# First loads on one queue in order of need, epsilon of the norms on VectorE, another order in the last norm

## The chip, the cores and the metric

The kernel runs on one core of a Trainium2 chip. The metric is the device time of one execution in microseconds (us). The core has five instruction streams that run side by side and wait for one another by semaphores: PE (TensorE: weight loads and matmuls), DVE (VectorE), ACT (ScalarE), POOL (GpSimd) and SP (SyncE, which here only issues DMAs). ACT and POOL can issue DMAs too. All DMAs are carried by 16 DMA engines.

## The reference, cut to what matters

A network of two layers, float32, on 256 tokens of width 1024:

```python
def reference(x, ...):
    for l in range(2):
        mix = mixer_sublayer(x, ...)                 # proj = x @ w_in (1024 x 7696), three branches, w_branch, w_out
        x = layer_norm(ALPHA * x + mix, ln1_g, ln1_b)
        ff = square(relu(x @ w_ff1)) @ w_ff2         # 1024 x 4096 and back
        x = layer_norm(ALPHA * x + ff, ln2_g, ln2_b)
    return x

def layer_norm(x, g, b):
    xc = x - mean(x)
    return xc * rsqrt(mean(xc * xc) + 1e-5) * g + b
```

One of the three branches (the gMLP) has a layer norm of its own, over 512 columns, with the parameters `gmlp_ln_g` and `gmlp_ln_b`.

## The kernel before, in words

**Number format.** Each float32 product is made of three matmuls in a faster format (F32R). An operand is split into a rounded part `hi` and a rest `lo = x - hi`; the product is hi·hi + hi·lo + lo·hi. The split of a weight piece is one ACT instruction (`split_hi`, L115: `whi` <- raw) and one DVE instruction (`split_lo`, L120: `wlo` <- raw, `whi`); the split of the input is L975 on ACT and L976 on DVE (`split_x`, tile `actT`). ACT and DVE take their instructions strictly in the order in which the program writes them.

**Pieces and units.** All weights come as *pieces* of up to 128 x 1024 float32 (512 KB). A piece is loaded by one DMA on SP's queue (L106) into a ring of raw buffers (tile `wraw`, four of them, and in the beginning six more, tile `wearly`). A piece may be loaded once the piece that held its buffer has had its `lo` made. PE's work is a list of *units*, each of which uses one or two pieces; a plan fixes at which unit the `hi` and the `lo` of each piece are written into the streams of ACT and DVE.

**The first nine units** (`first_units`) multiply the input with the columns for `v` and `gv`, 1024 columns in all: 8 steps over k (128 rows of the weights each), 12 matmuls of 512 columns in each step (two outputs, two token tiles, three products). In step 0 the weights come as two pieces of 256 KB, in the others as one of 512 KB. In this text w0 to w8 are these nine pieces, x0 to x3 the four loads of the transposed input (`xT`; k = 0, k = 1, k = 2 and 3, k = 4 to 7; 128, 128, 256 and 512 KB). x0 to x3 are issued by ACT, w0 to w8 by SP. The splits stand in this order: on ACT x0, w0, w1, x1, w2, x2, w3, w4, x3, w5 to w8; on DVE x0, w0, w1, x1, x2, w2, w3, x3, w4 to w8. So of step 1 the `lo` of w2 stands behind both parts of x2.

PE begins with `keep_warm` (L136): nine float32 matmuls of 128 columns on zeros, which need no load. The profile counts each as two.

**Parameters.** `params_a` (L309 to L320) loads what a layer's gMLP and GLA branches need: `lngb` (the norm's g and b and a bias, one row of 1536 sent to all 128 partitions, 768 KB), `ws` (512 KB), `bg` (2 KB) and `nw` (64 KB). POOL issues them: for layer 0 as `start` of unit 1, for layer 1 as `start` of the unit near the end of layer 0 that first uses the last weights of w_ff2. They are first needed at L344 (`lngb`, DVE, after unit 8), L351 (`ws`) and later.

**Norms.** `residual_norm` makes the sum with the residual (L227) and the statistics (L228, L231) on DVE; then `rstd_of` adds epsilon (L208) and takes the power -0.5 (L209), both on POOL; meanwhile DVE makes (x - mean) * g in two halves (L235), and then, when the power is there, the product with it plus b (L243). The last norm of the program, for the second token tile, treats columns 768 to 1023 apart: ACT multiplies (L240) and POOL adds b (L241), so that three output DMAs are issued, two by SP and one by ACT (L245).

```python
    load_xT(0)            # L1047
    load_more(1)
    load_xT(1)
    load_more(2)
    for c in (2, 3):
        load_xT(c)
    load_more()
    splits(-1)
```

Of the kernel before, what the change touches and what calls it, by code (L numbers as in the profile page):

```python
# [14 lines left out]
OP = mybir.AluOpType  # L15
# [6 lines left out]
NT = 2  # L22
# [12 lines left out]
EARLY_PIECES = 20  # L35
SPLIT_BUFS = 9
LEAD = 7
WARM = 9


class Piece:
# [13 lines left out]
def block_kernel(ctx, tc, ins, out):  # L55
    nc = tc.nc
# [5 lines left out]
    def sbt(tag, width, name, bufs=1, dt=F32):  # L62
        if width % 128:
            return small.tile([128, width], dt, tag=tag, name=name, bufs=bufs)
        return sb.tile([128, width], dt, tag=tag, name=name, bufs=bufs)
# [4 lines left out]
    def v3(t, n):  # L70
        return t.rearrange("p (a b) -> p a b", a=n)
# [11 lines left out]
    xraw = [sbt(tag, D, "xraw") for tag in ("Rk", "Rq")]  # L83

    def load_xT(c):
        k0, k1 = XCH[c]
        nc.scalar.dma_start(v3(xraw[k0 // 4], 4)[:, k0 % 4:(k1 - 1) % 4 + 1, :], ins["xT"][:, k0:k1, :])


    pieces = []  # L90
    units = []
# [6 lines left out]
    def start_load(p):  # L98
        n = p.shape[0] * p.shape[1]
        r = rank[id(p)]  # L100
        if r < EARLY_PIECES and r % (RAW_BUFS + EARLY_RAW) < EARLY_RAW:
            c = r % (RAW_BUFS + EARLY_RAW) * 1024
            p.raw = v3(early[:, c:c + n], p.shape[0])
        else:
            p.raw = v3(sbt("wraw", 1024, "wraw", bufs=RAW_BUFS)[:, :n], p.shape[0])
        nc.sync.dma_start(p.raw, p.src)  # L106
# [26 lines left out]
    def keep_warm(n):  # L133
        warm = pbank("pw", "warm")
        for _ in range(n):
            nc.tensor.matmul(warm[:, :128], wtile, wtile, start=True, stop=True)  # L136

    keep_warm(WARM)
    ident = sbt("ident", 128, "ident")
# [13 lines left out]
    def late_consts():  # L153
        nc.gpsimd.memset(wgx.bitcast(F32), 0.0)
        nc.gpsimd.memset(lrx.bitcast(F32), 0.0)
        nc.gpsimd.memset(scan_mask, 1.0)
        for n in range(4):
            nc.gpsimd.memset(scan_mask[:, n * 64:n * 64 + 1], 0.0)
        nc.gpsimd.memset(moba_mask[:, 128:256], 1)
        yield  # L160
        for h in range(H):
            nc.vector.tensor_scalar(gla_mask[:, h * 128:(h + 1) * 128], jp, 0.0, None, op0=OP.is_ge)
            nc.vector.memset(gla_mask[0:64, h * 128 + 64:(h + 1) * 128], 0)
        for c0 in (0, 256):
            nc.vector.tensor_scalar(moba_mask[:, c0:c0 + 128], jp, 0.0, None, op0=OP.is_le)
        yield
# [38 lines left out]


    def rstd_of(dst, var, eps, n=1):
        nc.gpsimd.tensor_scalar(dst, var, eps, None, op0=OP.add)  # L208
        nc.gpsimd.tensor_tensor(dst, dst, half_c.to_broadcast([128, n]) if n > 1 else half_c, op=OP.pow)  # L209

    def transpose_split(src, dst_hi, dst_lo, t, half):
        p = pbank("pw", "pT")
        for k in range(4):
            nc.tensor.transpose(p[:, k * 128:(k + 1) * 128], src[:, (half * 4 + k) * 128:(half * 4 + k + 1) * 128], ident)  # L214
        sl = (slice(None), slice(half * 4, half * 4 + 4), slice(t * 128, (t + 1) * 128))
        nc.scalar.copy(dst_hi[sl], v3(p, 4))
        nc.vector.tensor_tensor(dst_lo[sl], v3(p, 4), dst_hi[sl].bitcast(F32), op=OP.subtract)

    def residual_norm(t, acc, lnp, dst, final=False):

        g, b = lnp
        xr = xres[t]
        st = sbt("st", 12, "st", bufs=2)
        mv = sbt("mv", 3, "mvar", bufs=2)
        for h in range(2):
            sl = slice(h * 512, (h + 1) * 512)
            nc.vector.scalar_tensor_tensor(xr[:, sl], xr[:, sl], ALPHA, acc[h], op0=OP.mult, op1=OP.add)  # L227
            nc.vector.bn_stats(st[:, h * 6:(h + 1) * 6], xr[:, sl])  # L228
            if h == 0:
                yield  # L230
        nc.vector.bn_aggr(mv[:, 0:2], st)  # L231
        rstd_of(mv[:, 2:3], mv[:, 1:2], LN_EPS)
        for h in range(2):
            sl = slice(h * 512, (h + 1) * 512)
            nc.vector.scalar_tensor_tensor(xr[:, sl], xr[:, sl], mv[:, 0:1], g[:, sl], op0=OP.subtract, op1=OP.mult)  # L235
        last = final and t == NT - 1
        for c0, c1 in ((768, 1024), (0, 512), (512, 768)) if last else ((0, 512), (512, 1024)):
            sl = slice(c0, c1)
            if c0 == 768:
                nc.scalar.activation(xr[:, sl], xr[:, sl], AF.Identity, scale=mv[:, 2:3])  # L240
                nc.gpsimd.tensor_tensor(xr[:, sl], xr[:, sl], b[:, sl], op=OP.add)  # L241
            else:
                nc.vector.scalar_tensor_tensor(xr[:, sl], xr[:, sl], mv[:, 2:3], b[:, sl], op0=OP.mult, op1=OP.add)  # L243
            if final:
                (nc.scalar if c0 == 768 else nc.sync).dma_start(out[0, t * 128:(t + 1) * 128, sl], xr[:, sl])  # L245
        yield
        if final:
            return
        yield
        yield  # L250
        hi, lo, _ = dst()
        for h in range(2):
            transpose_split(xr, hi, lo, t, h)
# [50 lines left out]
    def build_layer(l, xT):  # L304
# [4 lines left out]
        def params_a():  # L309
            rs = sbt("RS", 1536, "lngb")  # L310
            a = ins["gmlp_rows"][l]
            nc.gpsimd.dma_start(rs, bass.AP(tensor=a.tensor, offset=a.offset, ap=[[0, 128], [1, 1536]]))
            ws = sbt("RkT", 1024, "ws")
            nc.gpsimd.dma_start(ws, ins["gmlp_wg"][l])
            bg = sbt("bg", 4, "bg")
            nc.gpsimd.dma_start(bg, ins["b_gate"][l])
            nw = sbt("nw", 128, "nw")
            a = ins["gla_norm_w"][l]
            nc.gpsimd.dma_start(nw, bass.AP(tensor=a.tensor, offset=a.offset, ap=[[0, 128], [1, 128]]))
            st.update(lng=rs[:, :1024], bs=rs[:, 1024:], wst=ws[:, :512], wgraw=ws[:, 512:], bg=bg, nw=nw)  # L320

        def params_ln(which):
# [9 lines left out]
        def gmlp_v_post(t):  # L332
            v = st["v"]
            vs = v[:, t * 512:(t + 1) * 512]
            nc.scalar.activation(vs, st["ps_v", t], AF.Gelu)
            yield
            for _ in range(t if l == 0 else 6 - 4 * t):
                yield
            s6 = sbt("st", 12, "st", bufs=2)
            mv = sbt("mv", 3, "mvar", bufs=2)  # L340
            nc.vector.bn_stats(s6[:, 0:6], vs)
            nc.vector.bn_aggr(mv[:, 0:2], s6[:, 0:6])
            rstd_of(mv[:, 2:3], mv[:, 1:2], LN_EPS)
            nc.vector.scalar_tensor_tensor(vs, vs, mv[:, 0:1], st["lng"][:, 0:512], op0=OP.subtract, op1=OP.mult)  # L344
            yield
            nc.vector.scalar_tensor_tensor(vs, vs, mv[:, 2:3], st["lng"][:, 512:], op0=OP.mult, op1=OP.add)
            st["v_done"] = st.get("v_done", 0) + 1
# [516 lines left out]
        def fin_of(which, dst, final=False):  # L864
            def fin(t, hf):
                if hf == 0:
                    st["fin", t] = residual_norm(t, st["acc", which, t], st[f"ln{which}"], dst, final)
                next(st["fin", t])
                if hf == 1:
                    side.append(st["fin", t])  # L870
            return fin
# [106 lines left out]
    xT = x0T  # L978
    sts = []
    for l in range(L):  # L980
        xT, s = build_layer(l, xT)
        sts.append(s)
    units[1].start = sts[0]["params"]
    units[6].start = lambda: side.append(late_consts())
    units[sts[0]["glb_unit"]].start = lambda: side.append(rope_tables())
    for s in sts:
# [34 lines left out]
    def load_more(limit=1000):  # L1021
        while loaded[0] < min(limit, len(pieces)) and taken_by[loaded[0]] < taken[0]:
            start_load(pieces[loaded[0]])
            loaded[0] += 1
# [15 lines left out]
    def advance():  # L1040
        for g in list(side):
            try:
                next(g)
            except StopIteration:
                side.remove(g)

    load_xT(0)  # L1047
    load_more(1)
    load_xT(1)
    load_more(2)  # L1050
    for c in (2, 3):
        load_xT(c)
    load_more()
    splits(-1)
# [54 lines left out]
```

## Time and profile before

| what | us |
|---|---|
| median of 3 runs | 880.16 (879.46 to 882.21) |
| the profiled execution's own time | 879.06 |
| its span (first to last instruction) | 877.3 |
| PE busy in the span | 863.3 (98%) |
| DVE, ACT, POOL busy | 616.8, 467.5, 73.9 |
| PE idle from 60 to 860 us | 0.65 (busy 799.35 of 800) |
| last matmul to the end of the span | 8.4 |

The span is cut into stretches by time; a row of a stretch gives, after its length, how long each engine was busy in it (and in how many instructions), TensorE's granted clock as a share of full speed (PEclk), the share of the DMA engines' time and the GB/s that they moved. A busy PE can still be slow: its matmuls are pipelined, so the distance from one start to the next says more. The timeline lists instructions by start; in brackets is how long the engine was idle before one, and what ended that.

### The profile page before, as it was taken

To read this page: it belongs to the slowest core of one execution; us is meant where nothing else is said; L and a number is where in the kernel's file an instruction comes from. 1 tells how busy PE (TensorE), PEld (TensorE's weight loads), DVE (VectorE), ACT (ScalarE), POOL (GpSimd) and SP (SyncE) were. 2 spreads that over 40 slices of the span, in tenths; PEclk is the share of its full clock that TensorE was granted. 3 is DMA by queue.
4 is the path that set the end of the run, shared out by engine and by line. 5 is a ranking of instruction groups with operands and counts; after the bars stand their busy time and mean duration, and the time that the engine had idled before them with its cause. 6 is when DMAs were issued, how large, how long until landed. Compare 5 with 4: busy or idle time off the path is not lost.

```text
span 877.3 us, 13105 instructions
## 1 busy us (share of the span) xinstructions
PE 863.3 (98%) x5022; PEld 752.3 (86%) x5022; DVE 616.8 (70%) x936; ACT 467.5 (53%) x768; POOL 73.9 (8%) x93
## 2 busy tenths in 40 slices
PE   7999999999999999999999999999999999999996
PEld 6898988889989888888889998878898988888884
DVE  4779799676787666666777867968677956666665
ACT  5657663567446544445354766645754555444440
POOL 1100000101511000000001100010042100000001
PEclk9999999999999999999999999999999999999999
DMA  9557764355557655556555765544467475555531
GB/s 336 185 159 227 238 197 144 112 161 184 192 196 241 232 190 192 190 192 216 168 163 154 216 195 165 174 138 145 144 213 222 150 233 192 191 192 192 192 121 48
DMA packets 118270, 162.10 MB, mean 185 GB/s; under 512 B 5248, under 2 KB 100000, under 8 KB 118208
## 3 DMA queue, kind: packets, MB, share of 16 engines
q1 hardware_dynamic: 116784, 157.34, 55.7%
q0 software_dynamic: 704, 2.76, 0.9%
q10 hardware_dynamic: 720, 1.18, 0.4%
q8 instruction: 39, 0.64, 0.3%
q14 instruction: 23, 0.19, 0.1%
HBM read 160.21 MB, written 1.05 MB: 184 GB/s over the span
## 4 chain that ended last, share of the span: by engine, by line
PE 92%; DMA 3%; DVE 3%; ACT 1%; issue 1%; POOL 0%; DVEq 0%; ACTq 0%; POOLq 0%; SPq 0%
PE pW L276 26%; PE acc L288 25%; PE pF L276 17%; PE pB L264 8%; PE pF L288 4%; PE pSmv L288 3%; PE pSgv L288 2%; PE pSv L288 1%; DMA wearly<-in_w_in_dram 1%; PE pGG L288 1%; DVE wlo L120 1%; DMA wraw<-in_w_in_dram 1%; PE pkv L458 1%; ACT whi L115 1%; PE po L482 1%; PE pT L214 1%
## 5 line engine op out<-in xcount | busy, mean ns | idle before, releaser
L115 ACT CAST whi<-wraw 128x1024 fp32r<-128x1024 f32 (+1 forms) x281 | 282.8, 1039 | 132.3 <-DMA wraw<-in_w_ff_dram 63.4
L120 DVE TENSOR_TENSOR wlo<-wraw,whi 128x1024 fp32r<-128x1024 f32 (+1 forms) x281 | 334.2, 1224 | 19.4 <-ACT whi L115 19.3
L276 PE MATMUL pW<-actT,whi 128*128 128x512 f32 x704 | 248.2, 401 | 0.0
L276 PE MATMUL pW<-actT,wlo 128*128 128x256 f32 x704 | 182.9, 280 | 0.0
L288 PE MATMUL acc<-whi,h 128*128 128x512 f32 x512 | 163.3, 391 | 0.0
L276 PEld LDWEIGHTS pW<-actT,whi 128*128 128x128 f32 x704 | 128.0, 188 | 24.6
L276 PE MATMUL pF<-actT,whi 128*128 128x512 f32 x416 | 146.7, 397 | 0.0
L276 PEld LDWEIGHTS pW<-actT,wlo 128*128 128x128 f32 x704 | 132.8, 189 | 7.1
L288 PEld LDWEIGHTS acc<-whi,h 128*128 128x128 f32 x512 | 96.1, 188 | 19.0
L276 PE MATMUL pF<-actT,wlo 128*128 128x256 f32 x416 | 108.2, 281 | 0.0
L288 PE MATMUL acc<-wlo,h 128*128 128x512 f32 x256 | 99.7, 389 | 0.0
L280 DVE TENSOR_TENSOR fr<-pF,fr 128x256 f32<-128x256 f32 x52 | 21.9, 424 | 101.1 <-ACT fr L279 101.1
L276 PEld LDWEIGHTS pF<-actT,whi 128*128 128x128 f32 x416 | 76.5, 188 | 15.4
L276 PEld LDWEIGHTS pF<-actT,wlo 128*128 128x128 f32 x416 | 78.5, 189 | 4.4
L288 PEld LDWEIGHTS acc<-wlo,h 128*128 128x128 f32 x256 | 48.1, 188 | 10.0
L279 ACT COPY fr<-pF 128x256 f32<-128x256 f32 x52 | 19.1, 372 | 58.6 <-PE pF L276 58.6
L208 POOL TENSOR_SCALAR mvar<-mvar 128x1 f32<-128x1 f32 x12 | 9.4, 779 | 434.7 <-DVE mvar L231 386.3
L288 PE MATMUL acc<-whi,actT 128*128 128x512 f32 x128 | 40.3, 391 | 0.0
L288 PE MATMUL pF<-whi,actT 128*128 128x256 f32 x192 | 36.6, 286 | 0.0
L280 DVE TENSOR_TENSOR gates<-pW,gates 128x256 f32<-128x256 f32 x48 | 19.5, 420 | 18.1 <-ACT gates L279 17.7
L279 ACT COPY gates<-pW 128x256 f32<-128x256 f32 x48 | 16.9, 370 | 27.6 <-PE pW L276 27.6
L938 ACT CAST h<-fr 128x256 fp32r<-128x256 f32 x52 | 19.3, 407 | 21.5 <-DVE fr L937 21.5
(226 smaller groups left out, 1255.9 us busy)
## 6 DMA issues: line engine op xcount, KB each, us to landing
wraw<-in_w_ff_dram SPq DMA_DIRECT2D x128, 512.0 KB, 5.0
wraw<-in_w_in_dram SPq DMA_DIRECT2D x104, 512.0 KB, 4.3
wraw<-in_w_branch_dram SPq DMA_DIRECT2D x24, 512.0 KB, 4.1
wraw<-in_w_out_dram SPq DMA_DIRECT2D x16, 512.0 KB, 3.3
wearly<-in_w_in_dram SPq DMA_DIRECT2D x7, 512.0 KB, 10.9
wraw<-in_w_in_dram SPq DMA_DIRECT2D x6, 396.0 KB, 4.2
lng<-in_ln_g_dram SPq DMA_DIRECT2D x4, 512.0 KB, 5.6
lnb<-in_ln_b_dram SPq DMA_DIRECT2D x4, 512.0 KB, 7.6
```

What stands on the lines that cost most here:

```text
L115: nc.scalar.copy(p.hi, p.raw)
L120: nc.vector.tensor_tensor(p.lo, p.raw, p.hi.bitcast(F32), op=OP.subtract)
L208: nc.gpsimd.tensor_scalar(dst, var, eps, None, op0=OP.add)
L214: nc.tensor.transpose(p[:, k * 128:(k + 1) * 128], src[:, (half * 4 + k) * 128:(half * 4 + k + 1) * 128], ident)
L264: nc.tensor.matmul(o, w, a, start=start and i == 0 and j == 0, stop=stop and i == n - 1 and j == 2)
L276: nc.tensor.matmul(d, w, a, start=start and i == 0 and j == 0, stop=last and j == 1)
L279: nc.scalar.copy(dst, p[:, 256:])
L280: nc.vector.tensor_tensor(dst, p[:, :256], dst, op=OP.add)
L288: nc.tensor.matmul(o, a, w, start=start and j == 0, stop=stop and j == 2)
L458: nc.tensor.matmul(p[:, h * 128:(h + 1) * 128], kT4[rows, t, h, :], v4[rows, t, h, :], start=True, stop=True)
L482: nc.tensor.matmul(p[r, c], at4[:, t, h, r], v4[:, t, h, :], start=first and r.start == 0, stop=True)
L938: nc.scalar.copy(hi[:, i], rr[i])
```

## The change

Four things change, and the order of instructions on SP, ACT, POOL and DVE with them; PE loses one warming matmul and nothing else.

1. The four loads of the input go from ACT's queue to SP's, and are written between the weight loads: x0, w0, w1, x1, w2, x2, w3, w4, x3, w5 and so on.
2. `params_a` goes from POOL's queue to SP's; in layer 0 it is issued as `start` of unit 3 in place of unit 1.
3. In `rstd_of`, for all 12 uses, epsilon is added on DVE; POOL keeps the power.
4. In the last norm of the program L235 works in the pieces 768-1023, 0-511, 512-767 in place of two halves.

Also, `WARM` is 8 in place of 9.

```diff
-WARM = 9
+WARM = 8
 ...
     def load_xT(c):
         k0, k1 = XCH[c]
-        nc.scalar.dma_start(v3(xraw[k0 // 4], 4)[:, k0 % 4:(k1 - 1) % 4 + 1, :], ins["xT"][:, k0:k1, :])
+        nc.sync.dma_start(v3(xraw[k0 // 4], 4)[:, k0 % 4:(k1 - 1) % 4 + 1, :], ins["xT"][:, k0:k1, :])
 ...
     def rstd_of(dst, var, eps, n=1):
-        nc.gpsimd.tensor_scalar(dst, var, eps, None, op0=OP.add)
+        nc.vector.tensor_scalar(dst, var, eps, None, op0=OP.add)
         nc.gpsimd.tensor_tensor(dst, dst, half_c.to_broadcast([128, n]) if n > 1 else half_c, op=OP.pow)
 ...
         rstd_of(mv[:, 2:3], mv[:, 1:2], LN_EPS)
-        for h in range(2):
-            sl = slice(h * 512, (h + 1) * 512)
-            nc.vector.scalar_tensor_tensor(xr[:, sl], xr[:, sl], mv[:, 0:1], g[:, sl], op0=OP.subtract, op1=OP.mult)
+        for c0, c1 in ((768, 1024), (0, 512), (512, 768)) if last else ((0, 512), (512, 1024)):
+            nc.vector.scalar_tensor_tensor(xr[:, c0:c1], xr[:, c0:c1], mv[:, 0:1], g[:, c0:c1], op0=OP.subtract, op1=OP.mult)
 ...
         def params_a():
             rs = sbt("RS", 1536, "lngb")
             a = ins["gmlp_rows"][l]
-            nc.gpsimd.dma_start(rs, bass.AP(tensor=a.tensor, offset=a.offset, ap=[[0, 128], [1, 1536]]))
+            nc.sync.dma_start(rs, bass.AP(tensor=a.tensor, offset=a.offset, ap=[[0, 128], [1, 1536]]))
 ...                                                 (the same for ws, bg and nw)
-    units[1].start = sts[0]["params"]
+    units[3].start = sts[0]["params"]
 ...
-    load_xT(0)
-    load_more(1)
-    load_xT(1)
-    load_more(2)
-    for c in (2, 3):
+    for n, c in ((0, 0), (2, 1), (3, 2), (5, 3)):
+        load_more(n)
         load_xT(c)
     load_more()
     splits(-1)
```

On SP, the start of the program before (`wearly` and `wraw` are weight pieces in their order: w0 and w1 in the first row, w2 to w5 in the second, w6 to w8 in the third):

```order
L106 DMA wearly<-in_w_in_dram 128x512 x2
L106 DMA wearly<-in_w_in_dram 128x1024 x4
L106 DMA wraw<-in_w_in_dram 128x1024 x3
L106 DMA wraw<-in_w_in_dram 128x4x256
L106 DMA wearly<-in_w_in_dram 128x4x256 x3
L106 DMA wearly<-in_w_in_dram 128x3x264 x2
```

The same place of the changed program (`xraw` is the input):

```order
L87 DMA xraw<-in_xT_dram 128x256
L106 DMA wearly<-in_w_in_dram 128x512 x2
L87 DMA xraw<-in_xT_dram 128x256
L106 DMA wearly<-in_w_in_dram 128x1024
L87 DMA xraw<-in_xT_dram 128x512
L106 DMA wearly<-in_w_in_dram 128x1024 x2
L87 DMA xraw<-in_xT_dram 128x1024
L106 DMA wearly<-in_w_in_dram 128x1024
L106 DMA wraw<-in_w_in_dram 128x1024 x3
L106 DMA wraw<-in_w_in_dram 128x4x256
L106 DMA wearly<-in_w_in_dram 128x4x256 x3
L106 DMA wearly<-in_w_in_dram 128x3x264
```

The four loads of the input, which ACT issued, now stand between the weights. On SP, the rows of the changed program that follow (the parameters of layer 0, before issued by POOL as its first DMAs):

```order
L106 DMA wearly<-in_w_in_dram 128x3x264
L311 DMA lngb<-in_gmlp_rows_dram 128x1536
L313 DMA ws<-in_gmlp_wg_dram 128x1024
L315 DMA bg<-in_b_gate_dram 128x4
L318 DMA nw<-in_gla_norm_w_dram 128x128
L106 DMA wearly<-in_w_in_dram 128x3x264
```

They stand behind 14 weight pieces and in front of all others. On DVE, the end of the program before, from the last statistics on (`xr_67` is the second token tile):

```order
L228 BN_STATS st<-xr_67 128x6
L231 BN_AGGR mvar<-st 128x2
L235 SCALAR_TENSOR_TENSOR xr_67<-xr_67,mvar,lng 128x512 x2
L243 SCALAR_TENSOR_TENSOR xr_67<-xr_67,mvar,lnb 128x512
L243 SCALAR_TENSOR_TENSOR xr_67<-xr_67,mvar,lnb 128x256
```

The same place of the changed program:

```order
L229 BN_STATS st<-xr_67 128x6
L232 BN_AGGR mvar<-st 128x2
L208 TENSOR_SCALAR mvar<-mvar 128x1
L235 SCALAR_TENSOR_TENSOR xr_67<-xr_67,mvar,lng 128x256
L235 SCALAR_TENSOR_TENSOR xr_67<-xr_67,mvar,lng 128x512
L235 SCALAR_TENSOR_TENSOR xr_67<-xr_67,mvar,lng 128x256
L242 SCALAR_TENSOR_TENSOR xr_67<-xr_67,mvar,lnb 128x512
L242 SCALAR_TENSOR_TENSOR xr_67<-xr_67,mvar,lnb 128x256
```

DVE has the addition of epsilon (L208) more, and its first product stands in three pieces, the one that ACT waits for in front.

## Rows read from the trace of the kernel before

**Rows 1.** Stretches: us, busy per engine (instructions), PEclk, DMA share, GB/s

```profile
5.40:31.00 25.60, 21.88 (x81) 16.76 (x82) 13.91 (x23) 14.00 (x15) 0.00 (x0) 0.93 1.05 376
60.00:860.00 800.00, 799.35 (x4690) 697.72 (x4690) 569.82 (x862) 433.62 (x722) 61.20 (x66) 1.00 0.57 184
```

**Rows 2.** Waits of PE: who waited for whom, us in total, times, longest

```profile
PE pSv L288 <- DVE wlo L120: 3.0, 2, 2.1
...
PE pT L214 <- DVE xr L243: 0.2, 1, 0.2
```

**Rows 3.** Timeline of the start: start us, us, instruction, idle before it

```profile
1.04 4.21 PE L136 MATMUL warm<-warmt 128*128 128x128 f32 x18 [1.04 <-DVE warmt L131]
...
5.42 0.80 PE L288 MATMUL pSv<-whi,actT 128*128 128x512 f32 x1 [0.16 <-ACT whi L115]
...
9.03 0.39 PE L288 MATMUL pSgv<-whi,actT 128*128 128x512 f32 x1
9.07 1.05 ACT L115 CAST whi<-wearly 128x1024 fp32r<-128x1024 f32 x1 [2.60 <-DMA wearly<-in_w_in_dram]
...
12.74 0.50 PE L288 MATMUL pSv<-wlo,actT 128*128 128x512 f32 x1 [2.07 <-DVE wlo L120]
...
13.99 0.55 PE L288 MATMUL pSgv<-whi,actT 128*128 128x512 f32 x1
...
17.87 0.40 PE L288 MATMUL pSv<-wlo,actT 128*128 128x512 f32 x1
...
20.96 0.50 PE L288 MATMUL pSv<-wlo,actT 128*128 128x512 f32 x1 [0.88 <-DVE wlo L120]
```

**Rows 4.** The chain of waits: first piece behind unit 8

```profile
34.63 11.26 PE pW L276 x64
```

**Rows 5.** Stretches of the first loads, as rows 1

```profile
2.00:4.00 2.00, 2.00 (x12) 2.00 (x11) 0.00 (x0) 1.28 (x1) 2.00 (x5) 1.00 0.74 229
4.00:6.00 2.00, 1.84 (x7) 1.24 (x6) 1.03 (x2) 1.39 (x3) 1.16 (x8) 1.00 1.03 345
6.00:13.00 7.00, 4.17 (x14) 2.82 (x14) 2.94 (x5) 2.13 (x4) 0.00 (x0) 1.00 1.03 420
...
14.00:17.00 3.00, 3.00 (x9) 2.32 (x8) 1.23 (x1) 0.61 (x2) 0.00 (x0) 0.51 0.94 320
...
21.00:33.00 12.00, 12.00 (x53) 9.95 (x54) 6.68 (x15) 6.24 (x7) 0.00 (x0) 1.00 1.08 349
```

**Rows 6.** DMA queues, 6 to 13 us: POOL's, then SP's

```profile
q0 software_dynamic: 263, 1.25, 43.2%
q1 hardware_dynamic: 269, 0.97, 34.1%
```

**Rows 7.** DMA queues, 16 to 19 us: SP's alone

```profile
q1 hardware_dynamic: 345, 1.25, 102.0%
```

**Rows 8.** Timeline: first use of the gMLP norm's parameters

```profile
34.20 0.75 DVE L344 SCALAR_TENSOR_TENSOR v<-v,mvar,lngb 128x512 f32<-128x512 f32 x1
```

**Rows 9.** Stretch in which layer 1's first pieces are loaded, as rows 1

```profile
420.00:430.00 10.00, 10.00 (x51) 8.41 (x50) 5.45 (x10) 4.44 (x7) 0.00 (x0) 1.00 0.56 192
```

**Rows 10.** Timeline of the last norm, after the last statistics

```profile
870.63 1.42 DVE L235 SCALAR_TENSOR_TENSOR xr<-xr,mvar,lng 128x512 f32<-128x512 f32 x2
...
871.54 0.93 POOL L209 TENSOR_TENSOR mvar<-mvar,halfc 128x1 f32<-128x1 f32 x1
...
872.50 1.61 DVE L243 SCALAR_TENSOR_TENSOR xr<-xr,mvar,lnb 128x512 f32<-128x512 f32 x2 [0.46 <-POOL mvar L209]
873.09 0.75 POOL L241 TENSOR_TENSOR xr<-xr,lnb 128x256 f32<-128x256 f32 x1 [0.62 <-ACT xr L240]
```

**Rows 11.** DVE groups by shape: count, busy us, mean ns

```profile
L937 DVE SCALAR_TENSOR_TENSOR fr<-fr 128x256 f32<-128x256 f32 x52 | 19.5, 416 | 0.0
...
L243 DVE SCALAR_TENSOR_TENSOR xr<-xr,mvar,lnb 128x256 f32<-128x256 f32 x1 | 0.9, 946 | 0.0
...
L489 DVE TENSOR_SCALAR rs<-rs 128x8 f32<-128x8 f32 x2 | 0.3, 172 | 7.0 <-ACT osq L488 7.0
```

More of the change, by code (lines that the diff above doesn't have):

```diff
@@ L222, in residual_norm @@
         xr = xres[t]
+        last = final and t == NT - 1
         st = sbt("st", 12, "st", bufs=2)
@@ L232, in residual_norm @@
         rstd_of(mv[:, 2:3], mv[:, 1:2], LN_EPS)
-        for h in range(2):
-            sl = slice(h * 512, (h + 1) * 512)
-            nc.vector.scalar_tensor_tensor(xr[:, sl], xr[:, sl], mv[:, 0:1], g[:, sl], op0=OP.subtract, op1=OP.mult)
-        last = final and t == NT - 1
+        for c0, c1 in ((768, 1024), (0, 512), (512, 768)) if last else ((0, 512), (512, 1024)):
+            nc.vector.scalar_tensor_tensor(xr[:, c0:c1], xr[:, c0:c1], mv[:, 0:1], g[:, c0:c1], op0=OP.subtract, op1=OP.mult)
         for c0, c1 in ((768, 1024), (0, 512), (512, 768)) if last else ((0, 512), (512, 1024)):
@@ L311, in params_a @@
             a = ins["gmlp_rows"][l]
-            nc.gpsimd.dma_start(rs, bass.AP(tensor=a.tensor, offset=a.offset, ap=[[0, 128], [1, 1536]]))
+            nc.sync.dma_start(rs, bass.AP(tensor=a.tensor, offset=a.offset, ap=[[0, 128], [1, 1536]]))
             ws = sbt("RkT", 1024, "ws")
-            nc.gpsimd.dma_start(ws, ins["gmlp_wg"][l])
+            nc.sync.dma_start(ws, ins["gmlp_wg"][l])
             bg = sbt("bg", 4, "bg")
-            nc.gpsimd.dma_start(bg, ins["b_gate"][l])
+            nc.sync.dma_start(bg, ins["b_gate"][l])
             nw = sbt("nw", 128, "nw")
             a = ins["gla_norm_w"][l]
-            nc.gpsimd.dma_start(nw, bass.AP(tensor=a.tensor, offset=a.offset, ap=[[0, 128], [1, 128]]))
+            nc.sync.dma_start(nw, bass.AP(tensor=a.tensor, offset=a.offset, ap=[[0, 128], [1, 128]]))
             st.update(lng=rs[:, :1024], bs=rs[:, 1024:], wst=ws[:, :512], wgraw=ws[:, 512:], bg=bg, nw=nw)
```

## The prediction

> **What bounds the kernel now.** I read the stretches first. From 60 to 860 us PE is busy for all but 0.65 us [rows 1]: what lies between the start and the end of the program is matmul after matmul, and an edit there can win next to nothing. Between 5.4 and 31 us it is busy 21.88 of 25.60 us, and at a granted clock of 0.93 [rows 1]. The waits of PE say for whom: 3.0 us in two waits for the `lo` part of a weight, and only 0.2 us for a norm [rows 2]. So there are two places to win, the start and the 8.4 us behind the last matmul.
>
> In the start, the first matmul on data stands at 5.42 us, the chain's next part behind unit 8 at 34.63 [rows 3, 4]: 29.2 us for 8 x 12 = 96 matmuls. Without stalls 53 take 12 us, 0.227 each (21 to 33 us) [rows 5], so 96 take 21.8 and 7.4 us are lost. The starts in rows 3 show where. From 9.03 to 12.74 lies one matmul more; at 0.227 apart the third start would have been at 9.48, so 3.2 us go there, because w2 was only there at 9.07 (ACT waited for it) and its `lo` at 12.7. From 13.99 to 17.87 there are 10 distances, 3.88 us where 2.27 do: 1.6 us, at a granted clock near 0.51 (14 to 17 us) [rows 5], the lower level of 1.2 GHz. Another 1.0 us goes at 20.96, again for a `lo`. The rest, 1.5 us, is mostly the first matmuls, which run 0.43 us apart.
>
> Why w2 is late is in the DMA rows. From 6 to 13 us the engines move 420 GB/s, they are full [rows 5], but 1.25 MB of the 2.94 MB belong to POOL's queue, the parameters, which nobody wants before 34.20 [rows 6, 8]; SP's weights get 0.97 MB. It is the order that is bad, not the rate.
>
> **The start, step by step.** Removed from in front of the weights are 1.38 MB of parameters; and x3 (0.52 MB) now stands behind w4. The sum of bytes up to each load (1 MB = 10^6 bytes): x0 0.13, w0 0.39, w1 0.66, x1 0.79, w2 1.31, x2 1.57, w3 2.10, w4 2.62, x3 3.15, w5 3.67, w8 5.24. If the flow ramps up as before (0.50 MB moved by 4 us, counting 0.04 from the first 2 us; then 345 GB/s to 6 us, then 420) [rows 5], these bytes have passed at 3.7 us (w0), 6.3 (w2), 6.9 (x2), 8.2 (w3), 9.4 (w4), 10.7 (x3), 11.9 (w5), 15.6 (w8). One queue alone can do that: SP's moved 1.25 MB in 3 us, 417 GB/s [rows 7]. From the bytes to the semaphore I add 0.6 us, an estimate: before, SP's first load was used at about 4.8 us and its second at 5.5, some 0.5 to 0.8 behind their share of the flow.
>
> - *First matmul.* w0 at 4.3, plus 0.61 us for its rounding and 0.05 to get to PE: 4.95 against 5.42. The warming matmuls would stand in the way with nine: they end at 5.25 [rows 3]; eight end 2 x 0.234 earlier, at 4.78. That edit costs nothing and hides behind the wait for w0.
> - *Step 0.* 12 matmuls took 3.8 us from the first start to the end of the last distance (5.42 to 9.26) [rows 3]. I keep that: 4.95 + 3.8 = 8.7.
> - *Step 1.* From the landing of w2 to the first matmul with its `lo` it took 12.74 - 9.07 = 3.67 us [rows 3]; the order on ACT and DVE (w2, x2; x2, w2) is not changed, so that remains: 6.9 + 3.67 = 10.6. PE has done one matmul of the step by then and waits 1.6 us. This is the stall that stays. Eleven matmuls later it is 13.1.
> - *Steps 2 to 7.* 72 x 0.227 = 16.3. For that nothing may come late. w4's `lo` is the closest: x3 lands at 11.3, its two halves take 1.04 and 1.22 on ACT and DVE, then 1.22 for w4: about 14.9 against 16.0, when PE wants it. w5 needs 15.9 and is wanted at 18.7; the later ones have more room, since ACT and DVE need 1.05 and 1.22 us per piece and PE 2.72. So 29.4 against 34.63: **5.2 us**.
>
> Bounds of the unknown terms. All losses gone would be 7.4. If the flow stayed at the 229 GB/s of 2 to 4 us [rows 5] all through, w2 would land at 8.1 and x3 at 16.1, and the same sum, with PE waiting again in step 3, ends at 33.0: a gain of 1.6. I take 5.2, since rows 7 show one queue at full rate. The slow clock of 14 to 17.9 I leave out, since the engine waits less in front of it; its price is 1.6 us.
>
> **The parameters.** In layer 0 they stand behind w0 to w8 and five more pieces, 7.7 MB; at 420 GB/s to w8 and 349 behind it [rows 5], `lngb` (0.79 MB) is there at about 25.5 us. The first to need it, L344, stood 0.4 us ahead of unit 8's end [rows 4, 8], so now at about 29.0. Behind it on DVE waits the `lo` of the eleventh piece, which PE needs at 29.4 + 2.8. SP goes on past their four issues to pieces that PE wants after 40 us. Cover of 3.5 us, cost nothing. In layer 1 they are issued about 420 us, behind the fourth piece of that layer, in a stretch in which the DMA engines are 0.56 busy and move 192 GB/s [rows 9]: room for 1.38 MB in the 10 us, cost nothing; without that room it would be their 3.9 us of transfer at 349 GB/s.
>
> **Epsilon on DVE.** POOL's addition took 0.78 us and goes; on DVE it is one instruction of 0.17 us (its form of 128x8) [rows 11], 12 times. In the middle DVE is idle a quarter of the time, and the power is ready before DVE has made its first products, so L243 starts about 0.2 us earlier; PE waited 0.2 us once for that [rows 2]. I take 0.2, between 0 and 0.3.
>
> **The last norm.** Before, the power ended at 872.47, 0.42 us behind the end of the second L235 (872.05), and three instructions followed: DVE's 512 columns, POOL's addition, DVE's 256 columns, from 872.50 to 874.11 [rows 10]. DVE's 256 took 0.946 us beside POOL's addition, and 0.416 elsewhere [rows 11]: the two don't run at once. Now epsilon takes the first place, 870.63 to 870.80, then come the three products of 0.38 + 0.70 + 0.38 (starts apart), to 872.3; the power, 0.42 behind the first of them, is done by 871.7, and ACT and POOL can begin 0.8 us earlier. But DVE is free only at 872.3, and POOL's addition then falls on its two products. With the same 1.61 us it ends at 873.9, 0.2 earlier; with the three one behind the other, 0.72 + 0.75 + 0.42, at 874.2, 0.1 later. I take **0.1 us**, between a loss of 0.1 and a gain of 0.8 (all that POOL's chain gains). The Trainium skill (SBUF — State Buffer, Who interferes with whom) has a rule that speaks against this edit: DVE and GpSimd hold a shared port pair by an exclusive lock, and the loser "fully blocks". By that rule it is the 0.1 later; the 0.946 agrees with it, the 872.50 to 873.25 of the first product, which POOL's start at 873.09 didn't stretch, only in part.
>
> **Sum.** 5.2 + 0.2 + 0.1 = 5.5 us. Against the profiled execution's own 879.06 us (span 877.3 and 1.76 around it) that is 873.6. The median of the runs, 880.16, lies 1.1 higher, so I forecast **874.6**.
>
> **Rivals.**
> 1. *The clock falls all the same.* PE still waits 1.6 us in step 1, just behind a slow step 0, and before, the fall came 1.3 us behind such a stall [rows 3, 5]. For it: the pattern is the same. Against: the stall is half as long. Price 1.6: a gain of 3.9, 876.3. The Trainium skill (TensorE: Matmul & The Clock Gate, HAM oscillation) tells of matmul bursts between waits for DMA that each start at the low clock; that would be this rival, and the trace of before agrees as far as its slow stretch stands behind its longest stall.
> 2. *One queue fills more slowly.* The first loads go out one after another from one engine instead of three, and the flow stays near 229 GB/s for long. The gain is 1.6 in the start, 1.9 in all: 878.3. For it: nothing shows one queue alone before 14 us. Against: rows 7.
> 3. *The parameters become the wait.* SP issues in order, so `lngb` waits for every weight ahead of it, and L344 holds all later `lo` parts on DVE. PE needs the eleventh piece's `lo` at 32.2; L344 (0.75) and that `lo` (1.22) must go before, so a landing behind 30.2 costs one for one. At 35.7 the gain is gone; it decides against the change, by the bound below, from 38.3 on. At 38.5, 13 us behind my forecast, the sum is 2.8 us slower than before: 883. Against: the 3.5 us of cover.
>
> **How the numbers follow.** Forecast 0.58, rival 1 0.23, rival 2 0.14, rival 3 0.05. A measurement of this kernel tells 0.3% from no change, 2.6 us: faster is below 877.5, slower above 882.8. The forecast and rival 1 lie below (0.78 of their 0.81), of rival 2 0.02; same gets 0.15, slower 0.05. The range starts at 872.3, where all 7.4 us and the rest come back, and ends at 878.5, just beyond rival 2.
>
> **What would show it.** ACT's first wait for w2 ends near 6.9 us; PE's only long wait is one of about 1.6 us for w2's `lo`, at 9 to 10.6; PEclk is 1.00 after 8 us; pW begins near 29.4; POOL's queue carries nothing; L243 or its like follows the first products without a wait, and the last output is issued within 0.3 us of before, counted from the last matmul. Wrong it is if w2 lands after 8 us, if the clock row shows 0.5 behind the first steps, or if L344 waits for a DMA.

## The result and the profile after

The changed kernel takes 875.9 us (median of 4 runs, 875.05 to 876.51) against 879.96 us (4 runs, 879.46 to 882.21) of the kernel before in the same rounds: a ratio of 0.9948, with a 95% interval of 0.9935 to 0.9960. It is faster, as forecast, and 1.3 us above the forecast of 874.6. The profiled execution has a span of 874.0 us and its own time is 875.73.

The chain of waits of the changed kernel at the five places that cut the span (start us, us, what):

```profile
32.43 11.26 PE pW L275 x64
...
80.81 11.52 PE pB L263 x96
...
421.55 13.61 PE acc L287 x60
...
508.99 11.50 PE pB L263 x96
...
849.71 16.34 PE acc L287 x72
```

The same places of the kernel before, from the second on (the first is [rows 4]):

```profile
82.51 11.50 PE pB L264 x96
...
423.58 13.62 PE acc L288 x60
...
511.50 11.50 PE pB L264 x96
...
852.57 16.34 PE acc L288 x72
```

Their differences are the whole balance of the 3.3 us of span. The end of unit 8 comes 2.20 us earlier (34.63 to 32.43). From there to the first `pB` it takes 48.38 us instead of 47.88: 0.50 is lost again (what that is, see e9_plr_later). The next three stretches shrink from 341.07, 87.92 and 341.07 to 340.74, 87.44 and 340.72: 1.16 us. From the last `acc` group's start to the end of the span it was 24.73 and is 24.29: 0.44. The sum is 3.30.

The start, in stretches (columns as in [rows 1]), to be read beside [rows 1] and [rows 5]:

```profile
2.00:4.00 2.00, 2.00 (x12) 2.00 (x11) 0.34 (x1) 0.42 (x2) 0.55 (x6) 1.00 0.98 280
4.00:6.00 2.00, 2.00 (x6) 1.26 (x6) 1.27 (x3) 1.64 (x3) 0.00 (x0) 1.00 1.00 262
6.00:13.00 7.00, 4.42 (x18) 3.02 (x18) 3.51 (x5) 3.77 (x4) 0.00 (x0) 0.99 1.02 392
13.00:14.00 1.00, 1.00 (x4) 0.80 (x3) 0.00 (x0) 0.90 (x1) 0.00 (x0) 0.50 1.02 414
14.00:17.00 3.00, 3.00 (x10) 2.33 (x9) 2.82 (x3) 2.28 (x4) 0.00 (x0) 0.61 1.02 404
```

POOL's queue is gone: SP's alone carries 2.74 MB from 6 to 13 us, where SP's weights had 0.97 MB [rows 6]. But from 13 us on the granted clock is at 0.50, the lower of its two levels, and then at 0.61, which is mostly that level. Why PE stood still before that is seen in ACT's and DVE's timeline and in the matmul that waited:

```profile
7.58 1.05 ACT L115 CAST whi<-wearly 128x1024 fp32r<-128x1024 f32 x1 [1.68 <-DMA wearly<-in_w_in_dram]
9.15 0.62 ACT L974 CAST actT<-xraw 128x512 fp32r<-128x512 f32 x1 [0.52 <-DMA xraw<-in_xT_dram]
10.47 1.04 ACT L115 CAST whi<-wearly 128x1024 fp32r<-128x1024 f32 x1 [0.70 <-DMA wearly<-in_w_in_dram]
...
9.80 0.69 DVE L975 TENSOR_TENSOR actT<-xraw,actT 128x512 fp32r<-128x512 f32 x1 [3.27 <-ACT actT L974]
10.41 2.36 DVE L120 TENSOR_TENSOR wlo<-wearly,whi 128x1024 fp32r<-128x1024 f32 x2
...
11.68 0.50 PE L287 MATMUL pSv<-wlo,actT 128*128 128x512 f32 x1 [2.51 <-DVE wlo L120]
```

w2 is rounded from 7.58 to 8.63. Its `lo` could follow on DVE, which is idle, but x2's `lo` stands ahead of it, and x2 lands only at 9.13. So DVE begins w2's `lo` at 10.41, and PE stands 2.51 us for a `lo` whose own input was ready at 8.6. The matmuls behind that wait still run at full pace, 0.23 us apart; at 12.96, 1.3 us later, they fall to 0.43.

The tail, as [rows 10]:

```profile
867.77 0.15 DVE L208 TENSOR_SCALAR mvar<-mvar 128x1 f32<-128x1 f32 x1
867.84 1.53 DVE L235 SCALAR_TENSOR_TENSOR xr<-xr,mvar,lng 128x256 f32<-128x256 f32 x3
868.06 0.66 POOL L209 TENSOR_TENSOR mvar<-mvar,halfc 128x1 f32<-128x1 f32 x1 [7.24 <-DVE mvar L208]
...
869.29 1.61 DVE L242 SCALAR_TENSOR_TENSOR xr<-xr,mvar,lnb 128x512 f32<-128x512 f32 x2
869.34 1.28 POOL L240 TENSOR_TENSOR xr<-xr,lnb 128x256 f32<-128x256 f32 x1 [0.62 <-ACT xr L239]
```

DVE's last two pieces take the same 1.61 us as before, but POOL's addition, which ran 0.75 us beside DVE's second piece, now begins with the first and takes 1.28.

### The profile page after: what moved, and what is told of

Its sections match the earlier page's. It is cut to its first block, busy times and chain, and to the rows that moved or that the text cites. A ratio compares the mean times of both kernels' runs of the same rounds, so it can differ in the third digit from the quotient of the medians.

```text
span 874.0 us, 13093 instructions
## 1 busy us (share of the span) xinstructions
PE 861.6 (99%) x5020; PEld 751.7 (86%) x5020; DVE 617.2 (71%) x949; ACT 468.3 (54%) x768; POOL 59.5 (7%) x73
## 4 chain that ended last, share of the span: by engine, by line
PE 94%; DMA 2%; DVE 2%; ACT 1%; issue 0%; SPq 0%; DVEq 0%; ACTq 0%
PE pW L275 26%; PE acc L287 25%; PE pF L275 17%; PE pB L263 8%; PE pF L287 4%; PE pSmv L287 3%; PE pSgv L287 2%; PE pSv L287 2%; PE pGG L287 1%; DMA wraw<-in_w_in_dram 1%; DVE wlo L120 1%; PE pkv L457 1%; DMA xraw<-in_xT_dram 1%; PE po L481 1%; PE pT L214 1%; PE po L477 1%
## 5 line engine op out<-in xcount | busy, mean ns | idle before, releaser
L209 POOL TENSOR_TENSOR mvar<-mvar,halfc 128x1 f32<-128x1 f32 x12 | 10.9, 905 | 444.8 <-DVE mvar L208 444.8
```

## The experiments

All are measured in five rounds against the kernel before, whose median was 880.55 us in the rounds of e1_x_only to e4_lo_first, 880.3 in those of e6_tail_dve to e9_plr_later and 879.9 in those of e5_warm_gap, e11_eps_tail and e12_lo_first_only. Times from different rounds are best compared by their ratios to it.

**The input alone** (e1_x_only): the kernel before, with its input loads in SP's queue in the new order.

```diff
-        nc.scalar.dma_start(v3(xraw[k0 // 4], 4)...
+        nc.sync.dma_start(v3(xraw[k0 // 4], 4)...
```

> The kernel before with one part of the change: the four loads of the input go from ACT's queue to SP's, between the weights. Parameters stay on POOL's queue from unit 1 on, epsilon and the last norm as before. Theory (the parameters' bytes are what made w2 late): POOL's queue still takes about 0.43 of the flow from 6 to 13 us, so w2 lands at 8 to 9 us against 9.07, and unit 8 ends at 33.5 to 35 us against 34.63; whole time within 1.2 us of before (878.8 to 880.5). Rival (the order of the input and the weights is what counts): w2 and x2 land as in the changed kernel (7.6 and 9.1), unit 8 ends near 32.4, the time falls by about 2.2.

883.49 us, ratio 1.003 (1.0019 to 1.004): slower, which neither side expected. Its DMA queues from 6 to 13 us, to be held against [rows 6] and, below them, against ACT's queue in the kernel before:

```profile
DMA packets 835, 2.33 MB, mean 333 GB/s; under 512 B 135, under 2 KB 261, under 8 KB 835
## 3 DMA queue, kind: packets, MB, share of 16 engines
q1 hardware_dynamic: 567, 1.47, 60.5%
q0 software_dynamic: 268, 0.86, 39.6%
```

```profile
q10 hardware_dynamic: 253, 0.72, 25.6%
```

Weights and input have 1.47 MB in their one queue, where they had 0.97 MB in SP's and 0.72 MB in ACT's. The whole flow is 333 GB/s instead of 420 [rows 5]; POOL's parameters still take 40% of the time. w1 is rounded at 8.14 us (before: 5.53) and w2 at 12.43 (before: 9.07), the granted clock is 0.50 from 13 to 19 us, and unit 8 ends at 37.26. Why the flow is lower with these two queues, I did not settle.

**The parameters alone** (e2_params_only): behind the weights on SP, all else as before.

```diff
-            nc.gpsimd.dma_start(rs, ...   (and ws, bg, nw)
+            nc.sync.dma_start(rs, ...
-    units[1].start = sts[0]["params"]
+    units[3].start = sts[0]["params"]
```

> The kernel before with one part of the change: the parameters go from POOL's queue to SP's behind fourteen weight pieces; the input stays on ACT's queue. Theory (the bytes of the parameters made w2 late): w2 lands at 6.5 to 7.5 us, since x3 on the other queue takes part of the flow but 1.25 MB of parameters are gone; unit 8 ends at 31.5 to 32.9 us; the time falls by 1.7 to 3. Rival (order counts): w2 lands at 8.5 or later, because ACT's queue with 1 MB of input runs beside it, unit 8 ends at 34 or later, the time falls by less than 0.6.

877.13 us, 0.9955 (0.9942 to 0.9969); unit 8 ends at 32.18 us. The theory holds in its main point: this edit alone gives the whole of the change's gain in the start (32.43 with the input moved as well). Two of its numbers were missed: w2 is used only at 7.88 us, and the time fell by 3.4 us, not by 1.7 to 3; two of the six executions, at 874.75 and 875.54 with a mean granted clock of 0.998 instead of 0.996, are faster than the rest.

**Epsilon back on POOL** (e3_eps_back), in the changed kernel.

```diff
-        nc.vector.tensor_scalar(dst, var, eps, None, op0=OP.add)
+        nc.gpsimd.tensor_scalar(dst, var, eps, None, op0=OP.add)
```

> The changed kernel with epsilon added on POOL again, all else kept. Theory (from the two traces: three of the four norms in the middle held PE's transposes back, by 0.34, 0.49 and 0.34 us): from the end of unit 8 to the last matmul it takes 1.2 us longer than in the changed kernel, the end behind the last matmul 0.2 to 0.5 longer; whole time 1.2 to 1.7 us above the changed kernel. Rival (the prediction's term: PE waited 0.2 us once): 0.2 us in the middle, 0.1 at the end, the time the same within what can be measured. The start is the same for both (unit 8 ends near 32.4).

877.88 us, 0.9963 (0.9948 to 0.9977). That is 2.0 us above the changed kernel by the medians and 1.3 by the ratios (0.9963 against 0.9948), whose intervals overlap; what settles it is the profile. The three stretches of the middle are 341.05, 87.92 and 341.11 us: 1.18 more than with DVE's epsilon. The tail is 0.06 longer; so of its 0.44 the new order of the pieces has most. By accident this profile shows the same start at another clock:

```profile
13.00:17.00 4.00, 4.00 (x19) 3.33 (x18) 2.85 (x3) 3.26 (x4) 0.00 (x0) 1.00 1.02 405
...
30.83 11.28 PE pW L275 x64
```

Here PE had waited 2.1 us, the clock stayed at 1.00, and unit 8 ended at 30.83: 1.6 us before the changed kernel's 32.43, with the same code in the start. The first matmul with w2's `lo` stood at 11.71, against 11.68 in the changed kernel, so the 1.6 us lie behind it and are the clock's. Two of this kernel's six executions took 875.48 (the profiled one) and 875.77 us at a mean granted clock of 0.998, the other four 877.77 to 878.88 at 0.993 to 0.996.

**w2's and w4's `lo` first** (e4_lo_first), in the changed kernel, on DVE ahead of the input chunk's split that stood in front.

```diff
             split_hi(p)
+            if rank[id(p)] in (2, 4):
+                take_lo()
```

> The changed kernel, with the lo part of w2 written on DVE ahead of the split of x2, and that of w4 ahead of the split of x3 (before, each stood behind it). Theory (w2's lo waits on DVE for x2, which lands 1.5 us after w2): the first lo matmul of step 1 starts at about 9.95 us instead of 11.68. If the stall of 2.5 us is also what lets the clock fall, the granted clock stays at 1.00 from 13 to 17 us and unit 8 ends at 28.9 to 29.5; time 2.9 to 3.5 us below the changed kernel. Rival (the clock falls whether PE stalls for 2.5 or for 1 us here): the row of 13 to 17 us shows 0.5 to 0.6 again and unit 8 ends at 30.5 to 31; 1.5 to 2 us below. Second rival (PE's wait is for w3 and x2 anyway, so the stall only moves to step 2): unit 8 ends at 32 or later, no gain.

873.32 us (872.81 to 873.56), 0.9916 (0.9903 to 0.9929): better than both kernels. Unit 8 ends at 29.52, and from 6 us on PE has no gap and the granted clock no fall:

```profile
6.00:13.00 7.00, 7.00 (x23) 5.65 (x24) 4.55 (x6) 4.38 (x6) 0.00 (x0) 1.00 1.00 384
13.00:17.00 4.00, 4.00 (x19) 3.30 (x18) 3.83 (x4) 3.34 (x4) 0.00 (x0) 1.00 1.02 408
```

Not all of that is the edit's doing. In this profile the matmuls of step 0 stand 0.43 us apart from 6.5 to 9.1 us, the distance that they have where the clock column reads 0.50, though here it reads 1.00; step 0 so ends at 10.3 us, and w2's `lo` is there by then. In the four later kernels with the same order of splits (e6_tail_dve to e9_plr_later) step 0 ends at 8.7 to 8.9, PE waits 0.8 us for that `lo`, and the clock stays up all the same; unit 8 ends at 29.14 to 29.89.

**The same order, nothing else** (e12_lo_first_only): that edit in the kernel before.

> The kernel before with w2's and w4's lo on DVE ahead of the input chunk's split that stood before it, and nothing else; the parameters still come on POOL's queue beside the first weights. Theory: the bytes set this start; the matmul that waits for w2's lo goes from 12.74 to about 11.4 us, but w3's and w4's hi land as late as before (w3's at 13.07), PE waits there instead, and unit 8 ends 0 to 0.7 us earlier than 34.63; the time is 0 to 0.7 us below the kernel before. Rival: DVE's order is the whole of it, the parameters cost nothing: unit 8 ends 3 us earlier or more, by the wait of 3.0 us and the clock that then stays up, and the time is 3 us or more below.

877.89 us, 0.9974 (0.9965 to 0.9984), 2.0 below: neither side's number. Unit 8 ends at 32.67. The matmul that waits comes at 11.43 instead of 12.74, as the theory had it, and w3's rounding still begins at 13.06; but the granted clock was 1.00 from 13 to 17 us, and that gain I had left out. So bytes (34.63 to 32.18 in e2_params_only) and DVE's order (to 32.67 here) each cost about 2 us of the start, the clock's part included: e2_params_only still had the fall (0.78 from 13 to 17 us), and the two edits together, without the input's move (29.24 in e7_x_on_act, below), bring 1.0 us more than the two gains added.

**The gap filled** (e5_warm_gap): the changed kernel with work for PE in the stall.

```diff
+        if i == 2:
+            keep_warm(9)
```

> The changed kernel with nine warming matmuls more ahead of unit 2's, in the 2.5 us in which PE waits for w2's lo. Theory: the clock fell at 13 us because PE stood idle just before; with the gap filled it stays at 1.00 from 13 to 17 us in every execution, unit 8 ends at 30.8 us (30.83 in e3_eps_back, whose clock didn't fall) where the changed kernel's ended at 32.43, and the time is 1 to 1.6 us below the changed kernel's 875.9, so 874.3 to 874.9. Rival: the fall doesn't hang on the gap, the granted clock is 0.5 to 0.8 there again, and the nine matmuls hold unit 2 up besides: unit 8 ends at 32.4 us or later and the time is 876 or more.

874.12 us (873.94 to 874.37), 0.9932 (0.9919 to 0.9946). The nine run in the stall, unit 2 still gets its `lo` at 11.88, and the clock stays up:

```profile
8.39 2.17 PE L136 MATMUL warm<-warmt 128*128 128x128 f32 x18
...
11.88 0.50 PE L287 MATMUL pSv<-wlo,actT 128*128 128x512 f32 x1 [1.08 <-DVE wlo L120]
...
13.00:14.00 1.00, 1.00 (x6) 0.84 (x5) 0.10 (x1) 0.77 (x2) 0.00 (x0) 1.00 1.00 410
14.00:17.00 3.00, 3.00 (x15) 2.45 (x14) 2.57 (x3) 2.50 (x3) 0.00 (x0) 1.00 1.03 402
```

Unit 8 ends at 30.98. From the first `lo` matmul to there it takes 19.10 us, where the changed kernel took 20.75 and e3_eps_back 19.12. All five executions have a mean granted clock of 0.997 to 0.999, the changed kernel's four 0.995 or 0.996. The theory holds: PE's idleness is what the fall hangs on. Matmuls that compute nothing win 1.8 us by the medians.

**The last norm on DVE alone** (e6_tail_dve), in e4_lo_first: pieces of 512, 256 and 256 columns, none on ACT and POOL.

> The kernel of e4_lo_first, with the whole last norm on DVE: its last scaling is done in three DVE pieces (columns 0 to 512, 512 to 768, 768 to 1024), none on ACT and POOL. Theory: DVE and POOL hold each other up in the tail (with both at work DVE's last 256 columns took 0.95 us and POOL's 256 took 1.28 us, against 0.42 us for such a piece of DVE alone in the profile before), so DVE alone ends its last piece 0.1 to 0.2 us earlier; last matmul to end of span 7.7 us (7.88 in e4_lo_first), time 873.1. Rival: the two engines do overlap in the tail, and DVE, with one more piece to do, ends 0.3 us later: 8.2 us, time 873.6.

873.08 us (872.41 to 873.36), with last matmul to end of span 7.99 us against 7.88. The tail lies between the two forecasts (7.7 and 8.2), and the times overlap those of e4_lo_first: undecided. What can be read is that ACT and POOL win nothing measurable there: without them DVE ran its three pieces in 1.54 us, and with them its two in 1.61.

**The input back on ACT** (e7_x_on_act), in e4_lo_first.

> The kernel of e4_lo_first, but the input's loads go to ACT's queue as in the kernel before; the parameters stay behind the weights on SP, and w2's and w4's lo stand early. It asks what the input's move is worth by itself once the parameters are out of the way. Theory: two queues share the flow without regard to need, x3 comes in early and takes bytes from w2 and w3; unit 8 ends 0.3 to 1.5 us later than 29.52 us, time 873.6 to 874.8. Rival: the queues get their share apiece and two fill no worse than one, so that with the parameters gone the order makes no difference: unit 8 ends within 0.3 us of 29.52, time 873.3.

872.78 us (872.14 to 873.23), 0.9911 (0.9896 to 0.9926); unit 8 ends at 29.24. The rival is right: with the parameters away and DVE's order mended, the input's move is worth nothing. In the profiles the first matmul comes later (5.41 us against 5.19), x0 having landed at 4.43 instead of 3.23, and the two queues together move 418 GB/s from 6 to 13 us against 384; that these two cancel is my reading and was not tried apart.

**Nine warming matmuls** (e8_warm9), in e4_lo_first, `WARM = 9`.

> The kernel of e4_lo_first with nine warming matmuls instead of eight. Theory: the first real matmul waits for w0's hi and starts at 4.83 us in any case, and the eight end before it; a ninth (about 0.43 us at half clock, as the others) ends about when w0's hi is there or holds the first matmul up by at most 0.3 us, which unit 2's short wait for its weight (0.4 us) takes up: time within 0.3 us of 873.3. Rival: the ninth holds up PE for its whole length and nothing gives it back: 0.4 us more, 873.7.

873.0 us (872.53 to 873.52), the first matmul at 4.91: nothing measurable, as the theory had it. (The 4.83 us of the expectation is the changed kernel's first matmul; in e4_lo_first's profile it stood at 5.19.)

**`plr` later** (e9_plr_later), in e4_lo_first: one more `yield` ahead of the transposes `plr`.

> The kernel of e4_lo_first with one more yield ahead of the transposes plr, which then stand behind the next unit's 16 matmuls on PE. It asks where the half to whole microsecond goes that is given back between the end of unit 8 and the group pB x96. Theory: it is plr, which needs a PSUM bank that ACT and DVE empty late (the wait is 1.3 us in e4_lo_first, 0.8 in the changed kernel, 0.3 before); put later it finds the bank empty, and the stretch from the end of unit 8 to pB x96 falls from 48.88 to 47.7 us; time 872.2. Rival: the late bank is only the last link of a chain that begins at a late weight load (57.23 to 63.18 us); whatever stands next on PE meets the same wait, the stretch stays above 48.6 us, and the time is within 0.3 us of 873.3.

873.32 us. The wait did not go, it changed its name. PE's waits there, in e4_lo_first:

```profile
PE plr L731 <- DVE gates L279: 1.3, 1, 1.3
```

and with `plr` later:

```profile
PE pB L263 <- DVE gates L279: 1.2, 1, 1.2
```

The rival holds: whatever stands next on PE meets it, and from the end of unit 8 to the end of `pB` it takes 60.38 us in both. Followed back in e4_lo_first, the chain goes back to a weight load, and no PE work is on it from 57.2 to 75.2 us:

```profile
57.23 5.95 DMA wraw<-in_w_in_dram
...
74.70 0.43 DVE gates L279
...
75.18 0.39 PE plr L731 x2
```

So this wait hangs on loads, rounding and emptying of banks around 60 us (the load took 3.62 us before, 5.51 in the changed kernel), and the stretch from the end of unit 8 to `pB` is 47.6 us plus the wait. It does not follow the start: with the start unchanged the stretch is 48.28 us (e11_eps_tail, a wait of 0.7), with the start 5.4 us earlier 47.90 (e7_x_on_act, 0.3), and with one alike 48.88 (e4_lo_first, 1.3). So the 0.5 us that the changed kernel loses here is not shown to be the price of its earlier start. What sets the wait was not tried.

**Epsilon and last norm alone** (e11_eps_tail): the kernel before with these two edits.

> The kernel before with the epsilon on DVE and the last norm's new order of pieces alone; its loads, parameters and warming matmuls are as before. Theory: the two are worth 1.2 us in the middle (three stretches of 341.07, 87.92 and 341.07 us, which become 340.7, 87.4 and 340.7) and 0.4 us at the end (last matmul to end of span 8.39, which becomes 7.95): 1.6 us, time 1.6 us below the kernel before in the same rounds, the start unchanged (unit 8 ends within 0.3 us of 34.6). Rival: part of the middle's gain comes by way of the start (another phase of loads and splits), and the two alone give the forecast's 0.3 us.

878.12 us, 0.9978 (0.9969 to 0.9987): 1.80 below. The chain, with unit 8 ending at 34.68 as before:

```profile
82.96 11.50 PE pB L263 x96
...
423.69 13.61 PE acc L287 x60
...
511.13 11.50 PE pB L263 x96
...
851.85 16.34 PE acc L287 x72
```

340.73, 87.44 and 340.72 us: 1.17 gained in the middle; last matmul to end of span 8.02 against 8.39. The theory holds, independently of the start.

## Why the prediction came out right, and which of its terms did not

**The forecast's time** was right to 1.3 us, partly by luck. In terms of the profiled execution it was 873.6 and became 875.73: the start brought 3.0 less, 0.5 was lost behind it, the middle brought 1.0 more and the tail 0.3 more. And the 1.1 us added for the distance from the profiled execution to the median were 0.2 this time, which hides about 0.9 more. Rival 1's time, 876.3, lies nearer to the measured 875.9 than the forecast, and of the three signs of being wrong that the prediction names one came: the clock row shows 0.5 behind the first steps.

**The start, 5.2 forecast, 2.2 measured.** The cause was right: the parameters on POOL's queue (e2_params_only alone: 34.63 to 32.18). Two steps failed, one mis-sized and one left out.
- *From the bytes to the semaphore, 0.6 us.* w2 was used at 7.58, not 6.9; x2 landed at 9.13, not 7.5. By the bytes that had passed, if they pass in order, the distance was 1.0 us for w2 and 1.8 for x2 (1.31 MB by 6.5 us, 1.57 MB by 7.3). The 0.6 leaned on w0's use at 4.8 us, which in the kernel before is when ACT had finished x0, without a wait for the load. (A slip of the sum, w0's bytes at 3.7 us where its own flow gives 3.5, cost nothing: step 1 waits for w2 either way.) Since x2's split stands ahead of w2's `lo`, it is x2 that decides, and the step "from the landing of w2 to its `lo`", which I kept at 3.67 us, took 4.10. The stall was 2.5 us, not 1.6, and unit 8 would have ended at about 30.8, as e3_eps_back did, not 29.4.
- *The clock that I left out.* It fell: rival 1, with the price that it had, 1.6 us (32.43 against 30.83, and 20.75 against 19.12 counted from the first `lo` matmul). e5_warm_gap shows that it hangs on PE's idle time in the stall, and e3_eps_back that the same start has executions without a fall. The stretch's granted clock was 0.58 in one and 1.00 in the other, after waits of 2.5 and 2.1 us. What the Trainium skill (TensorE: Matmul & The Clock Gate, HAM oscillation) says, that matmul bursts between waits for DMA each start at the low clock, these traces bear out only in part: behind the wait of 2.5 us the clock fell, but 1.3 us into the matmuls, and behind the wait of 2.1 us it did not fall at all.

The stall was taken as fixed ("the order on ACT and DVE is not changed, so that remains"). That is true of the change; e4_lo_first shows that two lines undo it.

**The input's move** was counted as a gain (x3 behind w4). e7_x_on_act says it is none, and without the parameters' move it costs 3 us (e1_x_only). Rival 2, that one queue fills more slowly, is half right: 392 GB/s from 6 to 13 us, not 229 and not 420 (369 to 392 in the profiles of all the kernels with these loads).

**Parameters and rival 3.** `lngb` landed at 27.3 us (forecast 25.5), its first use was at 32.1 and waited for no DMA. Cost nothing, as forecast, in layer 1 too.

**Epsilon, 0.2 forecast, 1.17 measured.** Two steps failed. The first is "L243 starts about 0.2 us earlier". DVE had waited 0.46 us for POOL's power, as [rows 10] show for the last norm; in layer 0's first norm, for the second token tile, before and then after the change:

```profile
262.41 0.21 DVE L231 BATCH_NORM_AGGREGATE mvar<-st 128x2 f32<-128x12 f32 x1
...
264.53 1.41 DVE L243 SCALAR_TENSOR_TENSOR xr<-xr,mvar,lnb 128x512 f32<-128x512 f32 x2 [0.46 <-POOL mvar L209]
```

```profile
260.71 0.21 DVE L232 BATCH_NORM_AGGREGATE mvar<-st 128x2 f32<-128x12 f32 x1
...
262.35 1.41 DVE L242 SCALAR_TENSOR_TENSOR xr<-xr,mvar,lnb 128x512 f32<-128x512 f32 x2
```

From the statistics to the product with the power it took 2.12 us and takes 1.64: 0.48 earlier, and the same for the first tile (252.18 to 254.30 before, 250.49 to 252.13 after). The second is "PE waited 0.2 us once for that [rows 2]". I took the wait that the view puts down to DVE. The view of line L214 in the kernel before lists all that PE sat idle before these transposes:

```profile
its engine sat idle before it (us, times) until:
  PE pT L214: 0.7, 3
  PE pSv L288: 0.6, 1
  DVE xr L243: 0.2, 1
```

and after the change:

```profile
its engine sat idle before it (us, times) until:
  issue: 0.2, 1
```

The 0.7 and 0.6 carry the names of PE's own earlier work, so I passed over them. They were the same lateness: the normalised rows came late, behind POOL's 0.78 us, and PE paid between and ahead of the transposes. In all 1.3 us of idle time went, close to the 1.17 of the stretches. With epsilon back on POOL (e3_eps_back) the same three rows, 0.7, 0.6 and 0.2, are there again.

**The last norm, 0.1 forecast, 0.44 measured**, inside its bounds (−0.1 to 0.8). Counted from the start of the last `acc` group, DVE's first final piece began 0.35 us earlier (19.93 us behind it before, 19.58 after) and the 1.61 us behind it stayed, as in the sum without a further hold-up for DVE; the forecast had 0.2. Epsilon held L235 up by only 0.07 us there, not 0.17, and 0.09 came behind DVE's last piece. The hold-up itself is real, and it is in the 1.61 us of both kernels: DVE's last 256 columns took 0.95 us, and e6_tail_dve's three pieces without POOL took 1.54. POOL's 1.28 us where it had taken 0.75 agree in kind with the rule of the Trainium skill (SBUF — State Buffer, Who interferes with whom). Counted from the end of DVE's first piece, POOL's addition ends about 0.6 us later in both kernels (873.84 and 870.62), as if it had to wait for that piece. The power took 0.66 us instead of 0.93; that this helped is not shown, since DVE no longer waited for it.

**Eight warming matmuls**: no cost, and by e8_warm9 no gain.

## What to carry to other kernels

When an engine waits for data, look not only at the load that is late but at what stands ahead of the data's last step on its engine: here some 2 us of the start, with the clock that fell behind it, went to DVE waiting for a load that the waiting matmul did not need. When you price a wait that goes, take all the idle time ahead of the instructions concerned, whatever name the view gives it, and not only the row that names your engine. And moving loads into one ordered queue was worth something here only where it took bytes that nobody wanted yet out of the way; the queue by itself gave nothing.

## What the hardware showed that was not expected

- The same start code had a granted clock of 0.58 and of 1.00 from 13 to 17 us in two executions, worth 1.6 us. With the gap filled the runs lie within 0.43 us of each other (873.94 to 874.37), those of the changed kernel within 1.46.
- A load's semaphore came 1.0 us behind its share of the flow for w2 and 1.8 for x2, with several loads queued on SP, by the estimate above; 0.6 was assumed. That is one execution: with the same loads w2 was used at 7.20 us in e4_lo_first and at 8.08 in e5_warm_gap.
- In the first microseconds the clock column can read 1.00 while the matmuls stand 0.43 us apart, as they do where it reads 0.50 (e4_lo_first, 6.5 to 9.1 us): there the distance of the starts is the surer sign.
- The input in SP's queue beside POOL's parameters lowered the flow of 6 to 13 us from 420 to 333 GB/s. With one queue alone it was 369 to 392, with SP's and ACT's 418 (e2_params_only, e7_x_on_act).
